# A two-layer hybrid block: transfers of the recurrence on the Sync queue, modulation weights loaded ahead, score matmuls over half the rows, another table of fillers

## The chip, the cores and the metric

The kernel runs on one core of one Trainium2 chip. The time is in device microseconds (us), smaller is better; each figure below says whether it is the median of the runs shown or one profiled execution. All data is float32 in HBM at the start, and the result is one tensor of 512x1024 float32.

## The reference, cut to what matters

Two layers, each over 256 context rows and 512 latent rows of width 1024. The second layer gives out only the latent rows.

```python
def trunk_layer(x, xc, c, c_ctx, last, ...):
    mod   = silu(c) @ w_mod + b_mod            # 6 vectors of 1024 (shift, scale, gate, twice)
    mod_c = silu(c_ctx) @ w_mod + b_mod        # the same for the context rows
    proj  = (x * (1 + sc1) + sh1) @ w_in       # parts: RWKV 1024, S5 256, q 512, k 128, v 128
    yr = rwkv_mixer(...)                       # 4 heads of 64; a state of 64x64, forward and reversed
    ys = s5_mixer(...)
    ya = attention_mixer(...)                  # 8 heads, 2 of keys; a band of 3 blocks of 128 and the context, with a sink
    mix = concatenate([yr, ys, ya]) @ w_out
    x = layer_norm(ALPHA * x + gt1 * mix, ln1_g, ln1_b)
    h = x * (1 + sc2) + sh2
    y = hier_moe(h, ...)                       # 4 groups of 8 experts, 2 experts a row, 3 matrices of 1024x512 each
    x = layer_norm(ALPHA * x + gt2 * y, ln2_g, ln2_b)
```

The recurrence of `rwkv_mixer` goes through all 768 rows, once in each direction: `s = s * w_t - (s kk_t) b_t + v_t k_t`, `y_t = s r_t`.

## The kernel before, in words

A layer has four stages, and the program records them one after the other.

1. `input_side` projects the rows with `w_in` (`proj`, matmul on line 243) and runs the S5 part; the RWKV part, the queries, the keys and the values go to HBM (`cvd`, `qd`, `kvd`, `yd`).
2. The mixing stage, where the change lies. `rwkv` works on 6 tiles of 128 rows. `front(i)` (line 366) makes the features of a tile and stores them in HBM records (`rec` line 461, `atd` line 462); `back(i)` (line 464) transposes them (tiles `ar`, `bz`), multiplies them into 64x64 score blocks (`sc`, matmul on line 503) and stores those too; `inverse(b)` inverts triangular blocks of 32 for three tiles and both directions at once, on VectorE and GpSimd; `solve(i, d)` reads its pieces back and stores the rest of the record (lines 571 to 610). Then `step(n, d)` (line 614) goes through 12 chunks of 64 rows for both directions: it loads a record of 512 KB (line 625) and does two small matmuls (lines 631 and 640) that depend on each other through the state; `output` (lines 672, 676) and `finish` make the rows from it. The transfers of these functions are issued in part by SyncE (SP), in part by ScalarE (ACT), whose sequencer then does no arithmetic until they are out.
3. The end of the mixing stage: `mixing` multiplies S5's and attention's part by `w_out` (`part`, line 1582, 12 matmuls of 512 columns a tile), later adds RWKV's part (`norm`, line 1635), does the first layer norm and the router (`choose`, whose counting matmul over `r_A` is on line 1458), and sorts the rows by expert (`finish`).
4. The experts: `Weights.fetch` (line 1824) loads three matrices of 2 MB for each of 32 experts on SP, `ffn_up` (line 1762) and `ffn_down` (line 1786) use them. The first six matrices lie in memory that the mixing stage has to give up first. `combine` and the second layer norm end the layer.

Between its pieces `rwkv` calls `fill(at)`, at the places 'front' (5 calls), 'back' (6), 'inverse' (1), 'step' (11) and 'end' (1). What a call records there is in the table `FILL`, for each layer three numbers a call: so many pieces of attention, so many units of modulation, so many pieces of `mixing`. A piece of attention is one pair of heads of a query tile: `scores` (matmul on line 877 of queries with keys), the softmax, and for the piece before it `turn` (transposes) and `values`. There are 24 pieces in layer 0 and 16 in layer 1. A unit of modulation (`mod_unit`) loads 512 KB of `w_mod` (tile `wmod`, line 118, two buffers), multiplies it (line 127) and reduces four partial sums (lines 135, 139); layer 0's mixing stage has 48 units (32 of layer 0, 16 of layer 1), layer 1's has 32. The keys lie in `kz` with 64 rows of zeros for each half of the heads, so that each score matmul goes over 128 rows; `bz` has zeros for the same reason.

The engines' orders inside the mixing stage come from a scheduler that the language runs over what was recorded: the places named here set what it may choose from.

```python
with tc.issue_after(k.load.ins):
    for _ in itertools.islice(att, n):
        pass
for q, c0 in itertools.islice(units, m):
    mod_unit(k, q, mp, c0, 128)
for _ in itertools.islice(mixes, x):
    pass
```

## Time and profile before

| what | us |
|---|---|
| median of 3 runs (2893.8 to 2897.02) | 2894.11 |
| the profiled execution's own time | 2882.98 |
| its span, first to last instruction | 2881.2 |

Busy time in the span: TensorE's matmuls 2219.2 us (77%), its weight loads 1487.5 us (52%, beside the matmuls), VectorE 1185.8 us (41%), GpSimd 823.0 us (29%), ScalarE 523.3 us (18%). 691.34 MB moved, 240 GB/s over the span. The shares are averages over stages that differ: from 273 to 930 us the core is in the mixing stage of layer 0, from 930 to 1485 in its experts, from 1823 to 2312 in the mixing stage of layer 1, from 2312 to 2835 in its experts. PE is TensorE's matmul, PEld its weight load, DVE VectorE, POOL GpSimd; a name with q (SPq, ACTq) is an engine's sequencer, which issues transfers.

### The profile page before, as it was taken

How to read it: one execution, taken by the hardware profiler on the slowest of the kernel's cores; microseconds unless marked ns; L12 is line 12 of the kernel's file. 1: busy time of each engine (PE TensorE's matmuls, PEld its weight loads, DVE VectorE, ACT ScalarE, POOL GpSimd, SP SyncE). 2: the span in 40 equal slices, each digit the busy share in tenths (PEclk: the TensorE clock that was granted, in tenths of full speed). 3: DMA queues.
4: the chain of work that ended last, by engine and by line, in shares of the span. 5: the costliest groups of instructions: out<-in, count | busy, mean ns of one | idle time of the engine just before them, and what ended most of it. 6: DMA issues, size and time to landing. Idle time of an engine off the chain costs nothing. (4 is left out here: it accounts for less than half of the span.)

```text
span 2881.2 us, 43454 instructions
## 1 busy us (share of the span) xinstructions
PE 2219.2 (77%) x16189; PEld 1487.5 (52%) x16189; DVE 1185.8 (41%) x2830; ACT 523.3 (18%) x1264; POOL 823.0 (29%) x1131
## 2 busy tenths in 40 slices
PE   5898677789874978989955787677898488788882
PEld 4786445567432544555525675455555254454441
DVE  7872554665556100000016873456645711111113
ACT  3222233223001100001015222233110100000001
POOL 2651322431544011101016652333324510111002
PEclk8999788789986999999987898579699699999996
DMA  8334466665627899989974324446784589998995
GB/s 241 93 94 116 141 179 185 175 189 163 220 93 265 351 418 371 391 329 379 388 279 121 83 56 142 117 128 161 212 244 140 230 355 418 416 379 331 384 419 201
DMA packets 404797, 691.34 MB, mean 240 GB/s; under 512 B 134755, under 2 KB 310627, under 8 KB 388097
## 3 DMA queue, kind: packets, MB, share of 16 engines
q1 hardware_dynamic: 311808, 600.10, 58.1%
q10 hardware_dynamic: 78880, 64.32, 7.5%
q0 software_dynamic: 13792, 22.61, 2.1%
q8 instruction: 211, 3.46, 0.5%
q14 instruction: 106, 0.86, 0.1%
HBM read 607.98 MB, written 95.44 MB: 244 GB/s over the span
## 5 line engine op out<-in xcount | busy, mean ns | idle before, releaser
L1762 PE MATMUL b_m<-w,xT 128*64 128x256 f32 x4928 | 593.7, 396 | 128.8 <-DMA w<-in_expert_w_gate_dram 80.2
L1762 PEld LDWEIGHTS b_m<-w,xT 128*64 128x64 f32 x4928 | 391.9, 142 | 333.3 <-issue 148.0
L243 PE MATMUL b_m<-xT,win 128*128 128x256 f32 (+1 forms) x1416 | 275.8, 355 | 7.0 <-POOL xT L167 3.5
L243 PEld LDWEIGHTS b_m<-xT,win 128*128 128x128 f32 x1416 | 232.8, 202 | 41.0 <-POOL xT L167 4.4
L1786 PE MATMUL b_m<-w,aT 128*64 128x512 f32 x1024 | 231.0, 592 | 1.1 <-issue 0.6
L1775 DVE COPY aT<-b_m 128x256 f32<-128x256 f32 x64 | 27.2, 425 | 474.4 <-PE b_m L59 474.4
L1792 POOL DMA_INDIRECT yb<-y,dx x64 | 63.9, 998 | 419.7 <-DVEq L1907 245.2
L1786 PEld LDWEIGHTS b_m<-w,aT 128*64 128x64 f32 x1024 | 76.2, 137 | 117.3 <-issue 108.3
L1764 ACT ACTIVATE act<-b_m 128x256 f32<-128x256 f32 x64 | 24.6, 384 | 566.8 <-PE b_m L1762 566.8
L1765 DVE TENSOR_TENSOR act<-act,b_m 128x256 f32<-128x256 f32 x64 | 27.0, 422 | 233.5 <-PE b_m L1762 233.5
L877 PE MATMUL b_a<-kz,qb 128*128 128x128 f32 (+2 forms) x416 | 111.9, 415 | 8.2 <-ACT pr L898 6.1
L1582 PE MATMUL b_a<-wo,yt 128*128 128x512 f32 x240 | 112.4, 618 | 0.0
L1792 POOL DMA_INDIRECT yb<-yo,dx x13 | 12.9, 994 | 291.7 <-ACTq L1907 166.2
L127 PE MATMUL b_a<-wmod,cc 128*32 128x128 f32 x1280 | 64.2, 315 | 40.0 <-DMA wmod<-in_w_mod_dram 28.0
L877 PEld LDWEIGHTS b_a<-kz,qb 128*128 128x128 f32 x416 | 78.2, 237 | 32.2 <-issue 13.0
L59 PE MATMUL b_a<-idf,pr 128*128 128x128 f32 x320 | 58.4, 304 | 34.3 <-DVE pt L921 11.5
L503 PE MATMUL b_g<-ar,bz 128*128 128x128 f32 (+1 forms) x384 | 66.2, 337 | 11.7 <-ACT bz L495 11.6
L1855 POOL DMA_INDIRECT xg<-hd,ix x32 | 33.0, 1031 | 146.8 <-PE b_m L59 105.2
L503 PEld LDWEIGHTS b_g<-ar,bz 128*128 128x128 f32 x384 | 61.8, 248 | 22.3 <-ACT bz L495 18.0
L1582 PEld LDWEIGHTS b_a<-wo,yt 128*128 128x128 f32 x240 | 45.2, 196 | 51.2 <-issue 50.3
L127 PEld LDWEIGHTS b_a<-wmod,cc 128*32 128x32 f32 x1280 | 37.7, 122 | 58.0 <-DMA wmod<-in_w_mod_dram 29.9
L551 POOL TENSOR_TENSOR tl<-Bm,Xh 112x4 f32<-112x4 f32 (+13 forms) x112 | 38.0, 339 | 95.0 <-DVE Xh L552 53.7
(539 smaller groups left out, 3979.9 us busy)
## 6 DMA issues: line engine op xcount, KB each, us to landing
w<-in_expert_w_gate_dram SPq DMA_DIRECT2D x64, 2048.0 KB
w<-in_expert_w_up_dram SPq DMA_DIRECT2D x64, 2048.0 KB
w<-in_expert_w_down_dram SPq DMA_DIRECT2D x64, 2048.0 KB
wmod<-in_w_mod_dram SPq DMA_DIRECT2D x80, 512.0 KB
rec<-rec SPq DMA_DIRECT2D x40, 512.0 KB
win<-in_w_in_dram SPq DMA_DIRECT2D x16, 1024.0 KB
wmod<-in_w_mod_dram SPq DMA_DIRECT2D x4, 2048.0 KB
sca<-sc SPq DMA_DIRECT2D x24, 256.0 KB
```

The source lines that it names most:

```text
L59: k.nc.tensor.transpose(out, x, k.idf[r:r + n, r:r + n])
L127: nc.tensor.matmul(p[32 * g:32 * g + 32, :], k.cc[:, kk, :], wt[:, kk, :], start=kk < 4, stop=kk >= 4, tile_position=(0, 32 * g))
L243: nc.tensor.matmul(p[:, :n], wt[u][:, kk, j * 128:j * 128 + 128], xT[v][:, kk, c0:c0 + n], start=kk == 0 and q == 0, stop=kk == 7 and q == 2)
L503: nc.tensor.matmul(pv[:, cp, q, 0:n, :], bk[:, hp, q, cp].rearrange("p s t -> p (s t)"), ar[:, 0:n, cp, q, :], start=True, stop=True)
L551: eng.tensor_tensor(t[:, 0:n, j:32], Bm[:, r0:r1, j:j + 1].to_broadcast([112, n, w]), x.to_broadcast([112, n, w]), op=ALU.mult)
L877: nc.tensor.matmul(dst, qb[:, 2 * v + e, :], kz[:, v, r, 128 * keys[c][0]:128 * keys[f - 1][0] + 128], start=c == 0 or (c == 4 and r == 0) ...
L1582: nc.tensor.matmul(ps[h], y[:, kt, :], wo[:, kt, 512 * h:512 * h + 512], start=kt == 0, stop=kt == 5)
L1762: mm = nc.tensor.matmul(p[64 * h:64 * h + 64, 0:256], xT[:, kk, :], w[:, kk, 256 * h:256 * h + 256], start=kk == 0, stop=kk == 7)
L1775: k.nc.vector.tensor_copy(aT, pa[:, 0:256].rearrange("p (j x) -> p j x", j=2))
L1786: nc.tensor.matmul(py[64 * s:64 * s + 64, :], aT[:, j, 64 * h:64 * h + 64], wd[:, q, 512 * s:512 * s + 512], start=q == 0, stop=q == 3)
L1792: sc = nc.gpsimd.indirect_dma_start(out=yb, out_offset=bass.IndirectOffsetOnAxis(ap=dst, axis=0), in_=y, in_offset=None, bounds_check=3071 ...
L1855: return nc.gpsimd.indirect_dma_start(out=out, out_offset=None, in_=hd, in_offset=bass.IndirectOffsetOnAxis(ap=idx, axis=0), bounds_check= ...
```

## The change: what it does

- Every transfer of `front`, `back`, `inverse` and `solve`, and the two small ones of `mod_unit`, that ACT issued is issued by SP. The store of `x1` in `norm` goes from SP to GpSimd.
- `mod_unit` is split: `mod_load` issues the load, and `fill` computes the units that the call before it loaded and then loads its own (at most 4), into four buffers of `wmod` in place of two. The loads are ordered behind the last transfer of RWKV, `k.latest`, that was recorded before. At 'end' what is left is loaded and computed at once.
- `kz` and `bz` lose their zeros: the two halves of the heads lie in rows 0 to 63 and 64 to 127, a score matmul goes over 64 rows, the two halves alternate and write to different PSUM banks.
- `FILL` is new. Pieces of attention in layer 0's front, back, inverse and step calls: 5, 6, 4 and 9 before, 5, 9, 3 and 7 after; units of modulation there: 12, 18, 6 and 12 before, 8, 12, 2 and 21 after, and 5 at 'end'. In layer 1 units: 0, 12, 9 and 11 before, 0, 12, 2 and 16 after, and 2 at 'end'; attention is unchanged there. Pieces of `mixing`: before, 2 in the sixth step call and 5 (layer 1: 3) in each from the eighth on; after, 1 in each from the fourth on and 2 in each of the last (three in layer 0). `mixing` does 4 (layer 1: 3) `w_out` parts before its router, 2 before.
- `pt`, the turned probabilities, has buffers by size.

```diff
-def mod_unit(k, l, mp, c0, n, bufs=2):
+def mod_load(k, l, mp, c0, n, bufs=2):
+    wt = mp.tile([128, 8, n], F32, name='wmod', bufs=bufs)
+    k.nc.sync.dma_start(wt, k.a['w_mod'][l].rearrange("(p k) n -> p k n", k=8)[:, :, c0:c0 + n])
+    return wt
+def mod_unit(k, l, mp, c0, n, wt):
...
-    bz = [Fp.tile([128, 2, 2, 2, 2, 64], F32, name='bz%d' % j) for j in range(2)]
+    bz = [Fp.tile([128, 2, 2, 2, 64], F32, name='bz%d' % j) for j in range(2)]
...
-            for src, r, c, q in ((kh[:, d], 0, 0, nc.scalar), (bt[:, d], 64, 0, nc.scalar), (VT[i], 0, 256, nc.sync)):
-                q.dma_start(rec[z, :, r:r + 64, c:c + 256], src)
-            nc.sync.dma_start(atd[z, :, 0], at[:, d, :])
+            for src, r, c in ((kh[:, d], 0, 0), (bt[:, d], 64, 0), (VT[i], 0, 256)):
+                nc.sync.dma_start(rec[z, :, r:r + 64, c:c + 256], src)
+            k.latest = nc.sync.dma_start(atd[z, :, 0], at[:, d, :])
...
-                for hp in range(2):
-                    r_ = slice(64 * hp, 64 * hp + 64)
-                    A.copy(bk[r_, hp, :, :, 1 - s, :], pv[r_])
+                A.copy(bk[:, :, :, 1 - s, :], p[:, 256 * s:256 * s + 256].rearrange("p (q c t) -> p q c t", q=2, c=2))
...
+            for q in range(2):
+                for cp in range(2):
+                    for hp in range(2):
+                        r_ = slice(64 * hp, 64 * hp + 64)
+                        nc.tensor.matmul(pvs[hp][:, cp, q, 0:n, :], bk[r_, q, cp].rearrange("p s t -> p (s t)"),
+                                         ar[r_, 0:n, cp, q, :], start=True, stop=True)
...
-        b = k.bank() if nk > 4 else None
+        b = [k.bank(), k.bank()] if nk > 4 else None
...
+        for c, f in runs:
+            for r in range(2):
+                q = slice(64 * r, 64 * r + 64)
+                dst = aa[r][:, 128 * c:128 * f] if c < 4 else b[r][:, 0:128]
+                nc.tensor.matmul(dst, qb[q, 2 * v + e, :], kz[q, v, 128 * keys[c][0]:128 * keys[f - 1][0] + 128],
+                                 start=c == 0 or c == 4, stop=True, skip_group_check=True)
...
-    for _ in range(2):
+    for _ in range(4 if l == 0 else 3):
         ready.append(parts.pop(0))
         part(ready[-1])
...
-            nc.sync.dma_start(x1[r], t)
+            G.dma_start(x1[r], t)
...
-                    for q, c0 in itertools.islice(units, m):
-                        mod_unit(k, q, mp, c0, 128)
-                    for _ in itertools.islice(mixes, x):
+                    for x in loaded:
+                        mod_unit(k, *x)
+                    loaded.clear()
+                    while True:
+                        with tc.issue_after(k.latest.ins):
+                            for q, c0 in itertools.islice(units, min(m, 4)):
+                                loaded.append((q, mp, c0, 128, mod_load(k, q, mp, c0, 128, 4)))
+                        if m < 9 or not loaded:
+                            break
+                        for x in loaded:
+                            mod_unit(k, *x)
+                        loaded.clear()
+                    for _ in itertools.islice(mixes, x_):
                         pass
```

What this does to the engines' orders is shown at three places. In these rows xN is a count of like instructions in a row, and a number behind a name tells buffers apart.

The first is ACT in layer 0's features, from the exponentials of one tile's features (L437 to L442, L440 to L445 in the change) to the next tile's sigmoids or scores. Before:

```order
L437 ACTIVATE e_3114<-e_3114 128x512
L438 ACTIVATE e_3115<-b_f 128x512
L442 ACTIVATE e_3119<-b_f 128x512
L474 DMA vz_2629<-rec 64x2x256
L129 COPY mres<-b_a 128x128
L461 DMA rec<-av 2x64x256
L461 DMA rec<-kd 2x64x256 x2
L461 DMA rec<-av 2x64x256
L894 ACTIVATE sm<-sm 128x2
```

The change:

```order
L440 ACTIVATE e_3053<-e_3053 128x512
L441 ACTIVATE e_3054<-b_f 128x512
L445 ACTIVATE e_3058<-b_f 128x512
L897 ACTIVATE sm<-sm 128x2
L901 ACTIVATE pr,s_3091<-b_a,sm 128x256 x2
L939 COPY ob<-b_a 128x256
```

Five transfers stood between the features and the softmax's first exponential (`sm`); none does now, and they stand in SP's order.

The second is PE at the end of layer 0's mixing stage, where the counting matmuls of the first `choose` (`r_A`, `tri`, `oneb`), `w_out` parts (`wo`, `yt`) and the last step's matmul of direction 0 (`b_f<-sb,rec` on L631, L632 in the change) follow each other. Before:

```order
L1462 MATMUL b_a<-r_A,oneb 128x32
L1582 MATMUL b_a<-wo_6766,yt 128x512 x36
L59 MATMUL b_f<-idf,y 128x128 x2
L713 MATMUL b_f<-g_2613,gl_4058 128x256
L672 MATMUL b_g<-sb_7471,rec_7521 64x128 x2
L1635 MATMUL b_a<-wo_7610,yo 128x512 x2
L59 MATMUL b_f<-idf,y 128x128 x2
L1635 MATMUL b_a<-wo_7610,yo 128x512 x2
L631 MATMUL b_f<-sb_7542,rec_7798 64x128 x2
```

The change:

```order
L632 MATMUL b_f<-sb_7407,rec_7651 64x128 x2
L1398 MATMUL b_a<-hT,wr 64x128 x4
L1585 MATMUL b_a<-wo_6251,yt 128x512 x2
L1398 MATMUL b_a<-hT,wr 64x128 x4
L1585 MATMUL b_a<-wo_6251,yt 128x512 x2
L1401 MATMUL b_a<-sel_108,r_lt 128x36
L1585 MATMUL b_a<-wo_6251,yt 128x512 x8
L1461 LDWEIGHTS tri
L1461 MATMUL b_a<-r_A,tri 128x32
```

The last step stands ahead of the first `choose` and of the two `w_out` parts that remain, one of which follows here; before, it stood behind `choose` and 36 matmuls of three parts.

The third is SP at the same end, up to the first expert's matrices. Before:

```order
L1576 DMA yt<-yd 128x768
L1578 DMA xq<-in_x_dram 128x1024
L1663 DMA x_0<-q 128x1024 x2
L1824 DMA w_7902<-in_expert_w_gate_dram 128x4096
L1824 DMA w_7904<-in_expert_w_up_dram 128x4096
```

The change:

```order
L1579 DMA yt<-yd 128x768
L1581 DMA xq<-in_x_dram 128x1024
L117 DMA wmod<-in_w_mod_dram 128x8x128 x4
L1652 DMA hd<-h 128x1024
L117 DMA wmod<-in_w_mod_dram 128x8x128
L1827 DMA w_7880<-in_expert_w_gate_dram 128x4096
L1827 DMA w_7882<-in_expert_w_up_dram 128x4096
```

Five loads of modulation and one store of `hd` now stand ahead of the first expert's matrices; the stores of `x1` are gone from there.

## Rows read from the trace of the kernel before

**Rows 1.** By stretch: us; PE, PEld, DVE, ACT, POOL busy; PE's clock; DMA share; GB/s.

```profile
273.00:561.00 288.00, 200.22 (x1658) 138.41 (x1659) 149.81 (x380) 89.52 (x273) 99.76 (x195) 0.78 0.59 164
561.00:771.00 210.00, 183.31 (x1804) 132.80 (x1802) 119.85 (x311) 50.52 (x169) 60.69 (x113) 0.89 0.68 198
...
843.00:930.00 87.00, 36.11 (x177) 22.17 (x176) 59.67 (x151) 9.57 (x19) 48.13 (x39) 0.65 0.59 211
930.00:1485.00 555.00, 488.72 (x3554) 285.05 (x3554) 49.04 (x107) 53.44 (x108) 61.69 (x61) 0.98 0.90 363
...
1823.00:2038.00 215.00, 166.58 (x1408) 124.94 (x1408) 127.33 (x317) 73.80 (x230) 74.42 (x164) 0.76 0.52 141
2038.00:2211.00 173.00, 149.22 (x1444) 95.38 (x1441) 90.77 (x211) 27.68 (x93) 60.00 (x85) 0.90 0.78 227
```

**Rows 2.** Instructions of ACT in time, 344 to 360 us: start, us, instruction, [idle before].

```profile
348.47 0.50 ACTq L461 DMA_DIRECT2D rec<-av  x1
...
353.91 4.59 ACTq L461 DMA_DIRECT2D rec<-av  x1
358.55 0.20 ACT L894 ACTIVATE sm<-sm 128x2 f32<-128x2 f32 x1 [10.12 <-DMA rec<-av]
```

**Rows 3.** Waits of ACT, 255 to 930 us: us in total, times, longest.

```profile
ACT mres L129 <- issue: 11.9, 2, 7.5
...
ACT mres L129 <- DMA rec<-av: 0.8, 1, 0.8
```

**Rows 4.** The same, 1810 to 2320 us.

```profile
ACT sm L894 <- DMA inv_t<-itm: 14.1, 1, 14.1
...
ACT xa L607 <- DMA xt<-inv_t: 1.3, 1, 1.3
```

**Rows 5.** Costliest groups of PE, whole span: busy us, mean ns, idle before and releasers.

```profile
L1786 PE MATMUL b_m<-w,aT 128*64 128x512 f32 x1024 | 231.0, 592 | 1.1 <-issue 0.6 <-DVE aT L1775 0.5
L1582 PE MATMUL b_a<-wo,yt 128*128 128x512 f32 x240 | 112.4, 618 | 0.0
L877 PE MATMUL b_a<-kz,qb 128*128 128x128 f32 (+2 forms) x416 | 111.9, 415 | 8.2 <-ACT pr L898 6.1 <-DVE qb L831 0.7 <-ACT pt L921 0.7
L503 PE MATMUL b_g<-ar,bz 128*128 128x128 f32 (+1 forms) x384 | 66.2, 337 | 11.7 <-ACT bz L495 11.6
L127 PE MATMUL b_a<-wmod,cc 128*32 128x128 f32 x1280 | 64.2, 315 | 40.0 <-DMA wmod<-in_w_mod_dram 28.0 <-ACT pr L898 10.7 <-DVE kd L431 0.6
```

**Rows 6.** Instructions of PE in time, 755 to 935 us.

```profile
802.32 0.21 PE L1458 MATMUL b_a<-r_A,tri 128*128 128x32 bf16 x1 [14.17 <-DVE r_A L1446]
...
802.47 33.34 PE L1582 MATMUL b_a<-wo,yt 128*128 128x512 f32 x72
...
840.83 0.32 PE L631 MATMUL b_f<-sb,rec 128*64 128x128 f32 x1
...
890.65 0.19 PE L1458 MATMUL b_a<-r_A,tri 128*128 128x32 bf16 x1 [7.77 <-DVE r_A L1446]
...
929.84 5.53 PE L1762 MATMUL b_m<-w,xT 128*64 128x256 f32 x34
```

**Rows 7.** The same, 2085 to 2330 us.

```profile
2093.66 0.64 PE L127 MATMUL b_a<-wmod,cc 128*32 128x128 f32 x16
2094.24 0.70 PE L877 MATMUL b_a<-kz,qb 128*128 128x256 f32 x2
...
2137.55 18.29 PE L1582 MATMUL b_a<-wo,yt 128*128 128x512 f32 x42
```

**Rows 8.** Issues of SP in time: around 340 us, and 860 to 935 us.

```profile
340.01 8.72 SPq L118 DMA_DIRECT2D wmod<-in_w_mod_dram  x2
349.19 0.81 SPq L462 DMA_DIRECT2D atd<-e  x2
...
871.70 0.33 SPq L1824 DMA_DIRECT2D w<-in_expert_w_gate_dram  x1
```

More of the change, by code (lines that the diff above doesn't have):

```diff
@@ L517, in back @@
             A.copy(r1, p[:, 0:256])
[L518 removed]
+            k.latest = nc.sync.dma_start(atd[z, :, 1], r1)
     def dblk(ap, s0, q):
@@ L919, in turn @@
                     tr(k, p[:, 256 * c + 128 * r:256 * c + 128 * r + 128], pr[:, r, 128 * (c0 + c):128 * (c0 + c) + 128])
-            t = P.tile([128, 512], F32, name='pt', bufs=6)
+            t = P.tile([128, 256 * n], F32, name='pt%d' % n, bufs=4 if n == 2 else 2)
             (A.copy if c0 % 4 else V.tensor_copy)(t[:, 0:256 * n], p[:, 0:256 * n])
```

84 lines of the change are left out of this document (36 added, 48 removed).

## The prediction, made before the changed kernel was run

> **What bounds the kernel now.** I read the busy times by stretch first, because the shares of the whole span mix stages that have nothing in common. In the experts' stretch the DMA share is 0.90 at 363 GB/s and PE is busy for 488.72 of 555 us [rows 1]: the matrices are the limit there, and the change touches nothing in it. Whatever moves must move in the two mixing stages, 273 to 930 us and 1823 to 2312 us. If such a stage ends earlier, the next one starts earlier, and the end of the kernel follows.
>
> Inside the mixing stage no single engine is the bound. In layer 0's features, 273 to 561 us, PE is busy for 200.2 of 288 us, DVE for 149.8, ACT for 89.5, and DMA has a share of 0.59 [rows 1]. That is a chain of waits through engines that each work in order. In the steps, 561 to 771 us, PE is busy for 183.3 of 210 us at a clock of 0.89 [rows 1]: there PE nearly is the bound, and what it does for others delays the recurrence. At the end, 843 to 930 us, it is busy for 36 of 87 us [rows 1]: norms, router and sorting, one after the other.
>
> Then I looked at what the queues do to these chains. ACT's time line shows it issuing stores of records: from 348.5 us on, four stores, and the softmax's small exponential behind them starts at 358.55, after 10.12 us without arithmetic [rows 2]. One store alone took 4.59 us to issue [rows 2], so the issue is held back. The table of ACT's waits shows how much there is of this in layer 0: 16 rows that name an issue or one of the transfers that the change moves, from 11.9 down to 0.8 us, add up to 88.5 us [rows 3] (I left out four whose transfer stays where it is). In layer 1 there are 13, from 14.1 to 1.3 us, in sum 84.4 us [rows 4]. The groups of instructions give what each matmul costs [rows 5], and PE's time line what stands in whose way [rows 6, 7].
>
> **The change part by part**, against the profiled execution, 2883.0 us; the median shown, 2894.1, is 11.1 us above it.
>
> *ACT issues no more transfers of RWKV.* Of the 88.5 us, 42.4 us are rows where the waiting instruction belongs to RWKV's own features or solves (the rest are attention's and modulation's); of the 84.4 us, 38.3 us. Together 80.7 us is the upper bound, nothing the lower. While one tile's chain stands still, another tile's matmuls and vector work go on, since two tiles are under way at a time; I take half: **-40**.
>
> *Modulation loaded one call ahead.* PE idled 28.0 us in front of L127 because `wmod` had not landed [rows 5]; in the features and the first steps the unit loads and multiplies in one call. With the load a call earlier and four buffers this can all go (-28), or nothing comes of it where the recurrence waits for something else (0). Half: **-14**. Nine more units in layer 0's steps cost PE 9 x 64.2/80 = 7 us, and three pieces of attention that leave the steps save 3 x 111.9/40 = 8 us in score matmuls alone. I set the two against each other.
>
> *Score matmuls over 64 rows.* L877 and L503 keep their count and columns. If the two halves run side by side, each pair takes the time of one. The trace has no pair of row halves of this size. The nearest rows are column halves: 512 columns cost 231.0/1024 = 0.226 us where halves alternate (L1786), and 112.4/240 = 0.468 us over the full array (L1582) [rows 5]. So the bounds are 0 and half of 111.9 + 66.2, 89 us. I take full overlap in busy time, and 40% of it on the path, since L877 lies partly in the steps (PE at 183.3/210 and 149.2/173) and partly, like all of L503, in features where PE has idle time (200.2/288, 166.6/215) [rows 1]: **-36**. A rule speaks against part of it. PE's order goes from modulation on 128*32 tiles straight into scores on 128*128: the first ends at 2094.30 and the second starts at 2094.24 [rows 7], with no idle time between the two. The Trainium skill, TensorEngine Tiling (Array Packing), Key Properties, says that a change of tiling mode drains the engine, and the change adds about 130 such passages, two for each of 40 pieces of attention and 24 tile-directions of `back`. By the row they cost nothing; by the rule, at an estimated 0.2 us each (about one matmul's own latency), the sum would be 26 us worse. The measurement shows no drain at such a passage, so I leave it at nothing.
>
> *`w_out` in steps.* Before, three parts (72 instructions, 33.34 us) run in one piece from 802.47 us on, after a wait of 14.17 us for the first `choose`, and the last step's matmul of direction 0 stands behind them at 840.83 us [rows 6]. In the new order that step stands ahead of `choose`, two of these parts have gone into earlier steps, and the last runs in a gap of the end. So 33.3 us leave the path behind `choose`, and two parts of 11.1 us come into steps in which PE is busy 87% of the time; I let 13 of those 22 us count: -20. In layer 1 a piece of 18.29 us between two steps [rows 7] is cut up the same way, and most of it only moves: -6. Sum **-26**; bounds 0 and -50.
>
> *Modulation left for the end.* Five units in layer 0 and two in layer 1 are loaded after the last step, ahead of the first expert's matrices on SP; the fifth needs a buffer that PE gives up behind the counting matmul of the second `choose`, 890.65 us, where the first matrix went out at 871.70 [rows 6, 8]. The cover is the time until the first expert's matmul at 929.84 [rows 6]: the six matrices that are fetched ahead, 12.6 MB at 363 GB/s [rows 1], take 35 us, and 890.65 + 35 = 926. If this cover goes, because the end gets shorter, each us is paid. I take 4 us in layer 0 and 2 in layer 1: **+6**; bounds 0 and 19 for the difference of the two issues, twice.
>
> *SP takes 232 transfers* (by the code: six for each of 24 tile-directions, 20 of `ar`, 12 of `vz`, 32 of modulation, 24 of `inverse`). At the 0.4 us or so of an issue that nothing holds back (two `atd` in 0.81 us [rows 8]), SP works 94 us more in the two stages. It does no arithmetic, but it works in order too: a store that waits for its producer holds up the next tile's loads. That was so before, where two loads of `wmod` held `atd` back from 340.0 to 349.2 us [rows 8]; those holds go with four buffers, and others come. No row shows SP with all of it. Bounds: 0, and the 80.7 us that ACT's chain now pays. I take somewhat over a third: **+30**.
>
> *Small ones.* 48 fewer copies into `bz` and half as many rotations of keys take work from ACT and DVE; the second score bank and a second reduction in 16 pieces add some. Net **-4**.
>
> Sum: -40 - 14 - 36 - 26 + 6 + 30 - 4 = -84. The profiled execution would take 2799, and the median, 11 us above it, **2810 us**.
>
> **The rivals.**
>
> *No overlap of the row halves.* Then the 36 us are missing: 2846. For it: the overlap is shown for column halves only. Against it: the weight loads and the banks differ for the two halves, as they do in L1786.
>
> *The clock.* The granted clock is 0.78 where PE is busy for 200.2 of 288 us, and 0.65 where it is for 36 of 87 [rows 1]: it lies between its two levels of 1.2 and 2.4 GHz, the lower the more often PE pauses. With 63 us less in the features PE pauses more. If the clock fell from 0.77 to 0.66 there, the remaining 304 us of PE work would take 51 us more, 40% of it on the path, 20 us: 2830. That goes with the Trainium skill, TensorE: Matmul & The Clock Gate, which says that the throttled state is the default and that activity releases it; by that rule I would give 2830, and the trace agrees as to direction.
>
> *The matrices wait for modulation.* If the end gets shorter by the 20 us of `w_out` while the last loads stay behind the second `choose`, the first expert waits for its matrices: up to 19 us in layer 0 and some 6 in layer 1, 2835.
>
> *SP becomes the bound, and the kernel slower.* A load of `wmod` is 512 KB, 3.2 us at 164 GB/s [rows 1], and now stands in the same queue as every record. If SP falls behind by a whole filler call, two such loads lie ahead of each store and read-back of a tile: two exposures of 6.4 us for each of six tiles, 77 us in layer 0, and about 50 in layer 1 with fewer loads. 2810 + 127 = 2937. It decides once the 94 us more of issues and the waits between them fill SP's idle time. [...] Against it: layer 0's features have 10 fewer units beside them (and inverse 4 fewer), 7 MB less.
>
> *Nothing comes out.* If the waits only change places, the time stays at 2890: the change does what it says, but chains go on through DVE and GpSimd, of which it takes little.
>
> **How the numbers follow.** The sum: 0.55. No overlap: 0.13. The clock: 0.08. Matrices wait: 0.10. SP the bound: 0.10. Nothing: 0.04. The prediction is that of the likeliest, 2810 us. Its own range is 2755 (ACT's whole 80.7 us, and half of what SP costs) to 2850 (no overlap). For 8 in 10 the upper end goes to 2885: it takes in the first three rivals and the larger price of SP, and leaves out the slower case and the one without effect, 14 in 100, and a little below. The lower end is 2745, 10 us below the likeliest's own, for `w_out`'s bound. A measurement of this kernel can tell about 0.2%, 6 us, from no change; so faster 0.86, the same 0.04, slower 0.10.
>
> **What would show it.** Right: ACT's waits on issues and on RWKV's transfers gone from its table (88.5 and 84.4 us to under 20); L877 and L503 at about half their busy time, 90 us in sum; PE's idle time for `wmod` under 8 us; no piece of `w_out` over 12 us ahead of a step; the first expert's matmul of layer 0 near 870 us instead of 929.84, and layer 1's mixing stage some 30 us shorter; the experts' stretches unchanged. Wrong: SP's own waits ahead of `cvt` or `rec` that grow by more than 50 us, PE waiting for `rec<-rec` in the steps, or the first expert waiting for `w` after its tokens have come.

## The result, and the profile after

The changed kernel takes 2976.69 us (median of 4 runs, 2973.61 to 2982.01), the kernel before 2893.95 on the same chip: a ratio of 1.029, 95% interval 1.0268 to 1.0311. It is 83 us slower; I had forecast 2810. The profiled spans are 2881.2 and 2976.6 us, 95.4 apart, since the profiled execution before was 11 us quicker than its median.

First by stretch, to be read against [rows 1]. The stretches of the kernel after are cut at the same events: first front to step 0's first matmul, steps of direction g, the last 87 us before the first expert, layer 0's experts, and the first two for layer 1. Columns as in [rows 1].

```profile
273.00:588.00 315.00, 195.04 (x1553) 131.41 (x1555) 165.62 (x405) 87.28 (x266) 100.25 (x204) 0.70 0.50 136
588.00:837.00 249.00, 198.58 (x1788) 134.23 (x1787) 109.77 (x281) 41.67 (x138) 52.51 (x97) 0.80 0.62 189
904.00:991.00 87.00, 41.73 (x242) 24.28 (x242) 47.62 (x138) 9.08 (x21) 39.43 (x35) 0.67 0.59 213
991.00:1546.00 555.00, 487.57 (x3552) 283.82 (x3554) 48.87 (x106) 53.21 (x107) 61.66 (x61) 0.98 0.90 363
1884.00:2115.00 231.00, 152.53 (x1376) 110.26 (x1378) 129.13 (x326) 69.10 (x219) 68.02 (x154) 0.73 0.51 142
2115.00:2314.00 199.00, 159.25 (x1442) 101.83 (x1442) 93.94 (x225) 24.36 (x80) 74.60 (x102) 0.79 0.65 194
```

The experts are unchanged (487.57 us of PE in 555). What was 288 us to the first step is now 315, with less PE work in it (195.04, was 200.22) at a lower clock (0.70, was 0.78); the steps, 210 us, now 249. These marks, read from PE's time line, tell where the 95 us arise:

| mark, us | before | after | more |
|---|---|---|---|
| layer 0: last store of the features | 507.3 | 507.4 | 0 |
| first matmul of step 0 | 561.8 | 587.7 | 26 |
| last step of direction g | 775.6 | 836.6 | 61 |
| first expert's matmul | 929.84 | 990.89 | 61 |
| layer 1: last matmul of the features | 1989.7 | 2036.0 | 46 |
| first matmul of step 0 | 2037.7 | 2114.9 | 77 |
| first expert's matmul | 2312.4 | 2405.0 | 93 |

The features themselves lose nothing, in layer 1 they gain 15 us (46 us late, after a start that is 61 us late). The loss lies between the features and the first step, 26 and 31 us, in layer 0's steps, 35, and in layer 1 from the first step to the first expert, 16.

PE's groups, as [rows 5], of the kernel after (line numbers there are 1 to 5 higher):

```profile
L880 PE MATMUL b_a<-kz,qb 64*128 64x128 f32 (+2 forms) x416 | 82.9, 447 | 57.1 <-DVE qb L832 55.1 <-DVE mrow L146 1.5 <-DMA qb<-qd 0.4
L59 PE MATMUL b_a<-idf,pr 128*128 128x128 f32 x320 | 68.8, 372 | 48.0 <-ACT pr L901 42.7 <-DVE pr L909 1.9 <-DVE mrow L146 1.6
L132 PE MATMUL b_a<-wmod,cc 128*32 128x128 f32 x1280 | 65.6, 310 | 20.1 <-DMA wmod<-in_w_mod_dram 11.0 <-ACT pr L901 3.2 <-DVE pt L924 2.9
...
L503 PE MATMUL b_g<-ar,bz 64*128 64x128 f32 (+1 forms) x384 | 37.8, 338 | 6.8 <-ACT bz L495 6.3 <-ACT ar L486 0.5
...
L516 PE MATMUL b_g<-vz,sc 128*64 128x64 f32 x384 | 27.8, 287 | 67.8 <-DVE sc L507 33.3 <-DMA vz<-rec 26.7 <-DVE Xh L553 4.4
```

and two groups of the kernel before that were not shown:

```profile
L59 PE MATMUL b_a<-idf,pr 128*128 128x128 f32 x320 | 58.4, 304 | 34.3 <-DVE pt L921 11.5 <-ACT pr L898 10.6 <-DVE pr L906 5.6
...
L515 PE MATMUL b_g<-vz,sc 128*64 128x64 f32 x384 | 25.6, 258 | 14.1 <-DVE sc L506 6.8 <-issue 5.1 <-DVE sm L904 1.8
```

Read the last column. PE now idles 57.1 us ahead of attention's scores, 55.1 of it for `qb`, whose sources SP loads (8.2 before, [rows 5]); 67.8 ahead of L516, 26.7 of it for `vz`, now an SP load (14.1 before); 48.0 ahead of the transposes of `pr` (34.3). Ahead of modulation it idles 20.1 (40.0 before). Together 96.4 us more idle time in four groups, while PE's busy time over the span fell from 2219.2 to 2210.7 us.

ACT's issue stalls did go, as forecast. Of the rows in [rows 3] that name an issue one is left in its table of waits, 255 to 1000 us (17.1 us, at L518). The longest wait for a transfer in layer 1, 1870 to 2410 us, is new:

```profile
ACT cvt L378 <- DMA cvt<-cvd: 31.9, 1, 31.9
```

It is not ACT's transfer but a load of `cvt` on SP that went out late. The waits moved to SP. Two rows of SP's table before, 255 to 930 us:

```profile
SPq L118 <- PE b_a L127: 71.8, 19, 21.9
...
SPq L610 <- DVE W L608: 15.1, 4, 4.4
```

and of its table after, 255 to 1000 us:

```profile
SPq L117 <- PE b_a L132: 94.3, 9, 30.7
SPq L610 <- ACT xa L608: 62.8, 9, 12.1
...
SPq L611 <- DVE W L609: 24.8, 4, 23.1
```

and its time line in two places, a burst of the features from 343 us on and the way to step 0 from 534 us on:

```profile
343.07 2.39 SPq L464 DMA_DIRECT2D rec<-av  x1
345.50 3.03 SPq L464 DMA_DIRECT2D rec<-vt  x1
348.58 2.60 SPq L465 DMA_DIRECT2D atd<-e  x1
351.23 3.00 SPq L117 DMA_DIRECT2D wmod<-in_w_mod_dram  x2
354.27 2.44 SPq L477 DMA_DIRECT2D vz<-rec  x1
356.82 0.54 SPq L488 DMA_DIRECT2D rec<-ar  x1
...
534.19 0.58 SPq L577 DMA_DIRECT2D x<-inv_out  x1
546.97 0.39 SPq L610 DMA_DIRECT2D rec<-xa  x1
547.45 0.60 SPq L611 DMA_DIRECT2D rec<-W  x1
548.11 0.60 SPq L577 DMA_DIRECT2D x<-inv_out  x1
548.76 0.60 SPq L579 DMA_DIRECT2D xt<-inv_t  x1
555.01 0.38 SPq L610 DMA_DIRECT2D rec<-xa  x1
...
562.20 0.37 SPq L610 DMA_DIRECT2D rec<-xa  x1
...
571.82 0.60 SPq L611 DMA_DIRECT2D rec<-W  x1
...
573.69 0.49 SPq L850 DMA_DIRECT2D qb<-qd  x1
574.23 1.82 SPq L856 DMA_DIRECT2D qr<-qd  x4
...
576.56 1.31 SPq L117 DMA_DIRECT2D wmod<-in_w_mod_dram  x2
577.91 1.47 SPq L626 DMA_DIRECT2D rec<-rec  x2
```

In the burst the rows follow each other and SP's table of waits is empty (339 to 358 us), and one issue still takes up to 3.03 us. The DMA share is 0.25 from 340 to 346 us and 0.17 from 346 to 352, so busy DMA engines don't explain it; what does isn't shown. In the second place SP stands for 12 us, from 534.8 to 546.97, in front of a store whose producer, ACT's copy into `xa`, isn't done; loads of the next solves (`x`, `xt`) stand behind that store, and so on for four solves. The first load of a record goes out at 577.91, behind the outputs of four solves, the second inverse's loads, a query's loads and two `wmod`. Before it went out at 544.51. And the query's loads at 573.69 are what PE waits for: its scores at 584.74 have 13.74 us of idle time for `qb` ahead of them, and step 0's matmul stands behind them in PE's order.

### The profile page after: what moved, and what is told of

It is laid out like the page before. It is cut to its first block, busy times and chain, and to the rows that moved or that the text cites. A ratio compares the mean times of both kernels' runs of the same rounds, so it can differ in the third digit from the quotient of the medians.

```text
span 2976.6 us, 43375 instructions
## 1 busy us (share of the span) xinstructions
PE 2210.7 (74%) x16189; PEld 1466.1 (49%) x16189; DVE 1192.4 (40%) x2828; ACT 509.4 (17%) x1216; POOL 822.9 (28%) x1131
## 5 line engine op out<-in xcount | busy, mean ns | idle before, releaser
L880 PE MATMUL b_a<-kz,qb 64*128 64x128 f32 (+2 forms) x416 | 82.9, 447 | 57.1 <-DVE qb L832 55.1
L59 PE MATMUL b_a<-idf,pr 128*128 128x128 f32 x320 | 68.8, 372 | 48.0 <-ACT pr L901 42.7
L880 PEld LDWEIGHTS b_a<-kz,qb 64*128 64x128 f32 x416 | 50.0, 243 | 76.9 <-DVE qb L832 56.1
L59 PEld LDWEIGHTS b_a<-idf,pr 128*128 128x128 f32 x320 | 52.3, 193 | 57.6 <-ACT pr L901 46.3
L132 PE MATMUL b_a<-wmod,cc 128*32 128x128 f32 x1280 | 65.6, 310 | 20.1 <-DMA wmod<-in_w_mod_dram 11.0
L657 POOL TENSOR_TENSOR sn<-st,gc 128x128 f32<-128x128 f32 x44 | 25.2, 576 | 197.5 <-DVE st L648 186.8
L516 PE MATMUL b_g<-vz,sc 128*64 128x64 f32 x384 | 27.8, 287 | 67.8 <-DVE sc L507 33.3
L937 PE MATMUL b_a<-pt,vta 128*64 128x256 f32 x320 | 61.1, 483 | 5.3 <-DVE pt L924 4.6
```

Of the source, the lines that this page charges most:

```text
L59: k.nc.tensor.transpose(out, x, k.idf[r:r + n, r:r + n])
L132: nc.tensor.matmul(p[32 * g:32 * g + 32, :], k.cc[:, kk, :], wt[:, kk, :], start=kk < 4, stop=kk >= 4, tile_position=(0, 32 * g))
L516: nc.tensor.matmul(p[64 * cp:64 * cp + 64, 64 * h:64 * h + 64], sc[:, 0, cp, hp, q, :], vv[:, cp, 64 * h:64 * h + 64], start=True, stop=True)
L880: nc.tensor.matmul(dst, qb[q, 2 * v + e, :], kz[q, v, 128 * keys[c][0]:128 * keys[f - 1][0] + 128], start=c == 0 or c == 4, stop=True, ski ...
L937: nc.tensor.matmul(o[64 * v:64 * v + 64, 0:256], vt[:, keys[c][0], 64 * v:64 * v + 64], PT[v, c // 2][:, 256 * (c % 2):256 * (c % 2) + 256 ...
```

## The experiments

Each ratio is to runs of the kernel before on the same chip. Of the 232 transfers moved, 104 are the features' (`front`, `back`), 96 those of the inverses and solves, 32 modulation's. (Two expectations miscount: that of the first run says 232 where it puts back RWKV's 200, that of the run with one store says 84 for the 96.)

**Undo one part of the change.** The queue put back (such a line for each of RWKV's transfers that the change moved):

```diff
-        nc.sync.dma_start(rec[z, :, :, 512:640].rearrange("c p x -> p c x"), xa)
+        nc.scalar.dma_start(rec[z, :, :, 512:640].rearrange("c p x -> p c x"), xa)
```

> The changed kernel with RWKV's 232 transfers back on ACT's queue where they were (the two transfers of modulation stay on Sync). Theory 1, Sync's one queue: stores that wait for their producers hold up the next tile's loads and the first record's load; then layer 0's first step starts 25 us earlier (587.7 back to about 562), layer 1's 30 us earlier after the same shift, direction g's chain of steps takes 214 us instead of 249, and the time falls by 60 to 90 us, to 2887 to 2917. Rival, the filler table: the time falls by less than 20 us, 2957 or more, since the same fillers still stand ahead of the steps. Rival, a trade: ACT's stalls on issues come back (17 to 88 us in its table of waits) and eat up the gain, within 10 us of 2977.

Measured 0.9997 (0.997 to 1.0024): 85 us of 2895 come back with RWKV's 200 transfers alone, all of the loss; modulation's 32 stay on SP. Layer 0's step 0 starts at 543.3 us, 18 earlier than before the change.

Only the table's third column put back:

```diff
-    for _ in range(4 if l == 0 else 3):
+    for _ in range(2):
```

> The changed kernel with only the table's third column, the pieces of w_out and norm, as before (two, none, then five pieces per step, and two tiles ahead instead of four or three). Theory 2, the pieces of the end go out too slowly: the stretch from the last step of direction f to the first expert's matmul in layer 0 goes from 129 back to about 90 us, and the time falls by 30 to 45 us, to 2932 to 2947. Rival, Sync's queue alone: the last tiles of attention and of the recurrence arrive late for other reasons, and the time stays within 10 us of 2977.

Measured 1.0273 (1.0239 to 1.0307): no difference. Theory 2 falls. The whole table put back (`FILL` as before, and the loop of `fill` to serve it):

```diff
-                        if m < 9 or not loaded:
+                        m -= 4
+                        if m <= 0 or not loaded:
```

> The changed kernel with the whole table of fillers as before (attention, modulation and end), loads still one call ahead where a call has at most four units (a call of more loads four at a time, the last four ahead). If attention beside the features is what delays the fronts and the first step (PE waits for the softmax there, 48 us ahead of b_a<-pr where it was 34), the time falls by 60 to 95 us, to 2882 to 2917, more than with the end's column alone. If Sync's queue is what delays them, it falls only by what the end's column gives, 0 to 45 us, and layer 0's first step stays at 580 us or later.

Measured 1.0359 (1.0322 to 1.0397), slower still, which neither branch had; step 0 starts at 620.3 us. Attention beside the features, as the new table has it, isn't what delays the fronts.

**One part of the change alone**, on the kernel before. Its queue edit for RWKV's 200 transfers only:

> The kernel before with RWKV's transfers on Sync as the only edit (modulation's loads still two buffers deep, unit by unit, in the same queue). If one in-order queue is the cause by itself, as in the run that put them back (74 us), this costs 50 to 100 us: 2945 to 2995. If it only hurts together with the new order of fillers and loads, it costs under 25 us, and if my prediction's sum was right without them it gains 10 us: 2884 to 2919.

Measured 1.0318 (1.0293 to 1.0344), 92 us slower. The queue alone does it, with the old table, buffers, keys and modulation. The keys and the block tile without zeros only:

```diff
-    kz = P.tile([128, 2, 2, T], F32, name='kz')
+    kz = P.tile([128, 2, T], F32, name='kz')
...
-                nc.tensor.matmul(dst, qb[:, 2 * v + e, :], kz[:, v, r, 128 * keys[c][0]:128 * keys[f - 1][0] + 128],
+                nc.tensor.matmul(dst, qb[q, 2 * v + e, :], kz[q, v, 128 * keys[c][0]:128 * keys[f - 1][0] + 128],
```

> The kernel before with only the keys and the block tile without zeros (score matmuls over 64 rows, two banks for the fifth key tile). By the prediction's term for the score matmuls, with the small ones: 2854 (minus 40), and L877's group of matmuls at about half its 111.9 us of busy time. If the halves don't overlap: 2890 to 2894. If each change of tiling mode costs a drain (130 passages at an estimated 0.2 us): 2880 or up to 2920.

Measured 1.0046 (1.0025 to 1.0067): 13 us slower instead of 40 faster. With the loads one call ahead in four buffers as well (and `pt` by size):

> The kernel before with the keys without zeros (whose room the four buffers need) and modulation loaded one filler call ahead in four buffers, with before's table and RWKV's transfers on ACT; to be compared with the keys alone, 2912. My term for the loads ahead was 14 us with bounds 0 and 28: 2884 to 2912, PE's 30.5 us idle for wmod under 10. Rival: before's table asks for more than four units in some calls, the load stands behind the step's record load by the new edge, and nothing comes of it: 2905 to 2920.

Measured 1.0067 (1.0044 to 1.009), no gain. PE still idles 25.1 us for `wmod`.

**Which transfers.** From the changed kernel, parts of the queue edit undone, by lines as in the first diff. The 96 of the second half (`itm`, `inv_out<-itm`, two of `inv_t`, `atl`, `xt`, `rec<-xa`):

> The changed kernel with only the solves' and inverses' transfers of the second half back on ACT (block loads, inverse stores, the solve's two loads, its first output); the features' transfers stay on Sync. With all of RWKV's transfers back the time fell by 74 us. If the hold is between the solves' outputs and the records' loads, this gives most of it: layer 0's first step at about 565 us instead of 588, steps some 30 us shorter, 2915 to 2935. If it is in the features, where a tile's stores stand in front of the next tile's loads, 2960 to 2980.

The 104 of the features (`rec<-kd`, `rec<-av`, `vz`, `rec<-ar`, `atd<-r`):

> The counterpart: the changed kernel with only front's and back's transfers back on ACT, the solves' and inverses' on Sync. If the hold is in the features, layer 0's features end some 12 us earlier than at 507 us and PE no longer waits for the read-back of v (15.5 us in one piece); 2915 to 2935. If it is between the solves' outputs and the records' loads, 2950 to 2970. If both parts count about alike, this and the run before each give 30 to 45 us, 2932 to 2947.

Measured 1.0054 (1.0028 to 1.0079) and 1.0202 (1.017 to 1.0235), 2915.56 and 2952.48 us: 68 and 25 us of the 85, as the second half's theory had it. In the first, the record load goes out at 549.1 us and step 0 starts at 559.0. So the second half carries most. Then one waiting store alone, the line of the first diff and nothing else:

> The changed kernel with one store alone, each solve's first output (rec from xa, 24 of the 232 transfers), back on ACT. If the 62 us that putting back the second half's 84 transfers gave come from this one store, which waits 62.8 and 54.8 us at the head of Sync's queue for ACT's copies while the next solve's loads and the records' loads stand behind it, the time falls by 40 to 62 us: 2915 to 2937. If they come from the solve's loads standing behind other stores, or from the number of transfers, it falls by less than 20 us: 2957 or more.

Measured 1.0272 (1.0247 to 1.0296), 5 us, within the intervals. My theory of the one store fell, and SP's table of waits of this kernel, 255 to 1000 us, shows what took its place:

```profile
SPq L611 <- DVE W L609: 69.0, 10, 17.6
```

The store beside it, which waited 24.8 us, now waits 69.0 in the same place. Both outputs off SP:

```diff
+        nc.scalar.dma_start(rec[z, :, :, 512:640].rearrange("c p x -> p c x"), xa)
+        nc.scalar.dma_start(rec[z, :, 64:128, 256:512].rearrange("c t x -> t c x"), W[64:128])
```

> The changed kernel with both outputs of each solve (rec from xa and from W, 48 transfers) on ACT; the solves' loads and the records' loads stay on Sync, with the features' stores. If loads that stand behind stores that wait for their producers are the cause, this gives most of the 62 us of the second half: 2915 to 2935, and layer 0's first record load goes out near 550 us instead of 577.9. If the length of the order of loads on Sync is the cause, or its place in the program's order, less than 20 us: 2957 or more.

The solves' loads off, the outputs left:

```diff
+        nc.scalar.dma_start(at, atd[z])
+        nc.scalar.dma_start(t[u:u + 32], inv_t[s0:s0 + 8].rearrange("h i t -> i h t"))
```

> The changed kernel with each solve's two loads (inverse, second half, and at with its product, 48 transfers) back on ACT, the outputs on Sync. If loads behind waiting stores are the cause, this gives part of the 62 us, since the records' loads still stand behind the outputs: 20 to 45 us, 2932 to 2957. If it is the number of issues of Sync, 48 of 232 give a fifth of 74 us, 15 us: 2962.

Measured 1.0211 (1.0178 to 1.0244), 23 us, 2953.67, between the two ranges that I had given, and 1.0281 (1.0253 to 1.031), nothing, above both of its. 48 issues fewer gave 23 us in one and nothing in the other, so the number of issues alone isn't the cause. Step 0 starts at 579.3 and 594.0. In both the record's load still stands behind the second inverse's and the query's loads. So I left everything on SP and wrote the records' loads earlier:

```diff
     solves(0, 0)
+    load(0)
+    load(1)
     solves(0, 1)
...
         steps((n,))
+        if n < 11 and n != 5:
+            load(n + 1)
```

> The changed kernel, every transfer on Sync as changed, with the records' loads written earlier in the program: those of steps 0 and 1 right behind the first solves, the others one step ahead, before the fillers' loads. If the place in Sync's order is the cause, the first record load goes out near 552 us instead of 577.9, layer 0's first step starts 15 to 25 us earlier, layer 1's too, and the time falls by 30 to 60 us: 2917 to 2947. If the steps are late because the solves themselves are late (their own loads and stores wait in turn), the loads go out early but PE waits for rec, and the time falls by less than 15 us: 2962 or more.

Measured 1.0266 (1.0241 to 1.0291). It did what was meant. SP's time line of this kernel (L624 is the record's load):

```profile
558.80 0.40 SPq L624 DMA_DIRECT2D rec<-rec  x1
...
579.64 0.57 SPq L863 DMA_DIRECT2D qb<-qd  x1
580.25 1.81 SPq L869 DMA_DIRECT2D qr<-qd  x4
```

and PE's (L649 is step 0's matmul, L893 attention's scores):

```profile
565.59 0.46 PE L649 MATMUL b_f<-rec 128*64 128x64 f32 x8 [0.34 <-DVE W L609]
...
571.61 0.63 PE L586 MATMUL b_g<-xt,ab 32*32 32x32 f32 x8 [4.10 <-DMA xt<-inv_t]
...
590.74 2.51 PE L893 MATMUL b_a<-kz,qb 64*128 64x256 f32 x16 [13.15 <-DVE qb L845]
```

The record load goes out 19 us earlier and step 0 starts 22 us earlier, at 565.59. But the query's loads now go out at 579.64 where it was 573.69, PE waits 13.15 us for them again, and behind them wait the next solves. Layer 0's last steps come earlier as well, direction g's by 19 us and f's by 25. But the first `choose` comes at 881.13 us where it was 880.35, and the first expert only 5 us earlier: the end of the stage didn't follow the steps, and what holds it wasn't tried. In layer 1 step 0 comes 23 us earlier and the first expert 8 later. So the time is as in my second case, though step 0 doesn't wait for `rec`. Neither this order nor any of the partial ones on one queue gave the time back.

**The rest of the change, without the queue edit.** RWKV's transfers on ACT; layer 1's row of the table and layer 0's third column as before (`range(2)`):

> The changed kernel with RWKV's transfers on ACT, layer 1's row of the table as before, and the end's pieces of layer 0 as before; keys without zeros, loads one call ahead and layer 0's attention and modulation as changed. If the 33 us that layer 1's mixing stage lost in the run with the queue put back come from the table, layer 1 returns to about 542 us of mixing and the time to 2860 to 2875, faster than before. If they come from the keys (the granted clock), it stays at 570 us and 2895 to 2905.

and with layer 1's row alone as before:

```diff
-        {'front': ((1, 0, 0),), 'back': ((0, 2, 0), (1, 2, 0)), 'inverse': ((1, 2, 0),),
...
+        {'front': ((1, 0, 0), (1, 0, 0)), 'back': ((0, 0, 0), (1, 4, 0), (1, 2, 0), (1, 2, 0)), 'inverse': ((1, 9, 0),),
...
-    for _ in range(4 if l == 0 else 3):
+    for _ in range(4 if l == 0 else 2):
```

> The changed kernel with RWKV's transfers on ACT and only layer 1's row of the table as before; layer 0 keeps the changed table, the end's pieces too. If the stages add up, layer 0 takes the 637 us of mixing of the run with the queue put back and layer 1 the 542 us of the mixed run: 2902 minus 33, 2869, the fastest so far. If layer 0's pieces only move the wait (its tail was 131.8 us after the last step where it was 86.8), 2885 to 2895.

Measured 0.9977 (0.9959 to 0.9994) and 0.9919 (0.99 to 0.9937). The second, 2872.73 us, is the fastest version and beats both kernels. Layer 1's mixing stage, first front to first expert, takes 541.7 and 541.4 us in the two, as expected, and 574.6 with the changed row (which of the row's columns costs it wasn't tried). The first version missed its 2860 to 2875 by layer 0, where the old third column takes 657 us of mixing and the new one 639.

With two modulation buffers and two loads ahead in place of four, and then with the zeros of the keys on top:

```diff
-                                loaded.append((q, mp, c0, 128, mod_load(k, q, mp, c0, 128, 4)))
-                        m -= 4
+                                loaded.append((q, mp, c0, 128, mod_load(k, q, mp, c0, 128, 2)))
+                        m -= 2
```

> The fastest version (RWKV's transfers on ACT, layer 1's row as before, keys without zeros) with modulation in two buffers, two loads ahead, as in the run with zeros (2920). If the zeros cost that run its 47 us, this stays near 2873, within 10 us. If the two buffers cost them, this is at 2905 to 2925 and the zeros cost nothing. PE's idle time for wmod tells how much of it the buffers are: 18.1 us in the fastest version, 28.3 in the run with zeros.

> The fastest version so far (2873: RWKV's transfers on ACT, layer 1's row as before) with the keys' zeros as before, so attention's score matmuls over 128 rows again; for the room, modulation in two buffers, two loads ahead. If the 64-row matmuls cost by the clock that PE is granted, as the keys alone did (13 to 17 us), this is faster: 2855 to 2865, with PE's clock in layer 0's features back from 0.74 to about 0.79. If they gain once PE is the bound of the steps, as my sum had it, this is 20 us slower: 2885 to 2900.

Measured 1.0041 (1.0025 to 1.0058) and 1.0089 (1.0055 to 1.0123). So in this setting four buffers are worth 35 us (PE idles 44.6 us ahead of modulation with two, 29.7 with four) and the keys without zeros 14, though the two intervals touch. My expectation of the run with zeros missed with both branches (2920.14 us), since I had put the two buffers at nothing; that of the two buffers came out, but for the zeros costing nothing.

All six parts of `w_out` in layer 0's steps, from the third filler call on:

```diff
-    for _ in range(4 if l == 0 else 2):
+    for _ in range(6 if l == 0 else 2):
```

> The same fastest version (keys without zeros, four buffers) with layer 0's six parts of w_out all in steps 2 to 7, so that none stands between the last step and the router. The tail after the last step of direction f is 133.6 us there and was 86.8 before; two parts of about 10 us each stand in it between two chooses that are 41 us apart. If those parts are the wait, the tail shrinks by 25 to 40 us, the steps grow by 10 to 20: 2850 to 2865. If DVE's and ACT's norms set the 41 us, the steps grow and the tail stays: 2880 to 2890.

Measured 0.9945 (0.9924 to 0.9966), no better than without. PE's time line of the fastest version, the three `choose` and the first expert:

```profile
810.01 0.21 PE L1461 MATMUL b_a<-r_A,tri 128*128 128x32 bf16 x1 [11.04 <-DVE r_A L1449]
...
852.58 0.18 PE L1461 MATMUL b_a<-r_A,tri 128*128 128x32 bf16 x1
...
894.08 0.21 PE L1461 MATMUL b_a<-r_A,tri 128*128 128x32 bf16 x1 [4.65 <-DVE r_A L1449]
...
917.22 8.02 PE L1765 MATMUL b_m<-w,xT 128*64 128x256 f32 x64
```

and of the version with six parts:

```profile
831.82 0.19 PE L1461 MATMUL b_a<-r_A,tri 128*128 128x32 bf16 x1 [5.01 <-DVE r_A L1449]
...
874.89 0.19 PE L1461 MATMUL b_a<-r_A,tri 128*128 128x32 bf16 x1 [13.23 <-DVE r_A L1449]
...
896.29 0.21 PE L1461 MATMUL b_a<-r_A,tri 128*128 128x32 bf16 x1 [4.65 <-DVE r_A L1449]
...
917.92 7.38 PE L1765 MATMUL b_m<-w,xT 128*64 128x256 f32 x60
```

The tail after the last step shrank from 133.6 to 98.5 us, but the steps grew by 35, and the first expert starts at the same time. In both it comes 22 to 23 us behind the third `choose`, right behind the copy into its tokens' tile `xT`, so it doesn't wait for its matrices. What sets the time of the third `choose` stays open.

Last, the price of score work by itself: every 64-row score matmul twice, on the kernel with the keys alone (and in `back` the loop over `q` as `(0, 1, 0, 1)`).

```diff
-        for c, f in runs:
+        for c, f in runs + runs:
```

> The keys-alone kernel with every score matmul over 64 rows issued twice (the second run overwrites the first's result), for PE's busy time of before without its waits. If the keys alone lost their gain to the granted clock (0.75 in the steps where it was 0.89, 0.69 in the features where it was 0.79) because PE has less to do, the clock here goes back above 0.85 in the steps and the time does not rise: 2895 to 2912. If the clock is low because matmuls over half the rows count for less, it stays near 0.75 and the time goes up by the added work on the path, 15 to 45 us: 2927 to 2957.

Measured 1.02 (1.0171 to 1.0229), 45 us slower than with the keys alone. A stretch of layer 0's steps that begins 10 us ahead of step 0, columns as in [rows 1], of the keys alone:

```profile
548.00:776.00 228.00, 195.34 (x1775) 137.47 (x1775) 110.77 (x307) 50.54 (x169) 57.13 (x112) 0.75 0.61 177
```

and of the doubled one:

```profile
561.00:800.00 239.00, 209.92 (x2036) 154.99 (x2036) 127.12 (x349) 56.77 (x188) 67.48 (x132) 0.81 0.63 187
```

Doubling adds 83 us of busy time (93.8 + 41.4 to 140.8 + 77.0), so 1 us of score work costs half a us on the path, near the 40% that I had taken. The granted clock was 0.89 before [rows 1], 0.75 with less score work, and 0.81 with more than before, where PE is busy for 209.92 of 239 us, as large a share as before: it came back half way. The time rose as the second theory had it, the clock did not do what either had, so neither is shown. What lowers it isn't settled, nor how much of the time it costs.

## Why the prediction was wrong

The steps of my sum, put beside a path from before to after in which each kernel adds one part:

| kernel | ratio | this part, us | predicted |
|---|---|---|---|
| keys and blocks without zeros | 1.0046 | +13 | -40 (scores, small ones) |
| and loads ahead, four buffers | 1.0067 | +6 | -14 |
| and layer 0's attention and modulation, `x1` on GpSimd | 0.9977 | -26 | 0 |
| and layer 0's `w_out` in steps | 0.9919 | -17 | -20 |
| and layer 1's row | 0.9997 | +23 | -6 |
| and the queue | 1.029 | +85 | -10 |

(The us are the difference of two ratios times 2895, uncertain by 6 to 10 us each. My +6 for modulation left for the end belongs to the rows of the table.)

*The queue: the step that failed.* I had set -40 for ACT against +30 for SP. Two things were wrong. First, "at the 0.4 us or so of an issue that nothing holds back": I took the quickest issues. Summed over the issues in the two mixing stages (255 to 930 and 1765 to 2312 us before, 255 to 991 and 1826 to 2405 after), SP spent 298 us before and 511 after, 213 more and not 94: 151 for the transfers that had been ACT's, 0.65 us each, and 62 more for those that were SP's already. ACT had spent 154 us on the same transfers, so the trace before had their price; its 4.59 us for one store [rows 2] I had charged to ACT alone. Second, the price of the waits: I bounded SP's loss by what ACT's chain pays, "0, and the 80.7 us", and took a third. A wait at the head of SP's queue holds loads of other chains (queries, records, `cvt`), which had stood on SP behind fewer such stores, so that upper bound wasn't one. How the 85 us divide between the longer issues and these holds isn't shown. The -40 was real in the table of waits and worth nothing in time: with the queue on ACT (0.9997) ACT's waits on issues and on these transfers are back, 52.2 us in 12 rows of its table in layer 0, and the kernel is 85 us faster. I had also read too much into that table: 16.4 of the 80.7 us are waits for transfers that SP issued before too (`rec<-vt`, `x<-inv_out`, `wmod`, `inv_out<-Xh`). The Trainium skill says in DMA: Bandwidth & Descriptors, Issuing engines are not separate DMA queues, that issuing on several engines saves only the sequencer's time to initiate, usually small. The runs differ from that: the same transfers on two engines are worth 85 to 92 us. In the trace an issue that waits holds back all that stands behind it on its engine, 12 us at 534.8; that such holds are all of the difference isn't shown.

*SP becomes the bound* was the rival with the right sign, at 0.10. Its mechanism was half right. On the way to step 0 no load of `wmod` waits; SP waits for ACT's `xa`, 26.8 us in layer 0 (507 to 588 us) and 28.1 in layer 1, and query loads stand ahead of the records. In layer 0's steps SP does wait 53.7 us in front of `wmod`, but that was 61.5 before; what is new there is 36.0 us for `xa`, and 24.3 for `W` where it was 15.1. Its 127 us, on top of 2810, were less than the 167 us by which the forecast failed, since the other gains failed too.

*Score matmuls.* The halves run side by side, as I had assumed, so *no overlap* falls: in 331 of the 400 pairs the second half starts within 12 ns of the first. At a granted clock of 1.0 (2.4 GHz) the next pair over 128 columns follows after 105 ns, where a full-row score matmul followed after 112; at 0.5 (1.2 GHz) the two are 207 and 213. Yet busy time fell only from 111.9 to 82.9 us (L880) and from 66.2 to 37.8 (L503), 57 us and not 89. Counted from start to start the two groups took 139.4 us before and 78.4 after; the rest, the last matmul of each run of them up to its end as the profile models it, stayed (39.0 and 42.8). So the term was too large in busy time because that last matmul doesn't halve, and little of it was gained on the path: nothing is seen on the kernel before (+13), and 14 us in the fastest version with two buffers. Of the rivals, the clock fell as it said: with the keys alone from 0.79 to 0.69 in the features (255 to 561 us; I had written 0.77 to 0.66) and from 0.89 to 0.75 in the steps. Of the steps from one of attention's 128-column score matmuls, or pairs, to the next 73 of 182 were slow ones (213 ns) before, 74 of 131 with the keys alone. Whether that is what cost the gain isn't shown.

The drain: I read "no idle time between" two modes as no cost. That was the wrong comparison. Over successive matmuls that overlap in the two mixing stages before, at a granted clock of 1.0, a full-array matmul over 128 columns is followed after 111 ns (median) if the next has the same tile size and after 203 if it has another; over 512 columns, after 429 and 522. At 0.5 it is 213 and 351, 854 and 991. So a change costs about 0.09 us, at the lower clock 0.14. The Trainium skill says in TensorEngine Tiling (Array Packing), Key Properties, that a change of tiling mode drains the engine; the trace agrees, with those 0.09 and 0.14 us. The price here is small: from one matmul to the next the size changes 587 times in the two stages before and 679 times with the keys alone, 92 times 0.09 to 0.14, 8 to 13 us, not 26.

*Modulation ahead.* Alone nothing, as its lower bound had it; together with the new row of layer 0, 35 us. (Of the 8 us that I had set against the nine more units, a third wasn't there: two pieces of attention leave the steps, not three.) *`w_out` in steps* was right for layer 0 (-17, forecast -20) and not for layer 1, whose row as a whole costs 23 us; PE's time line there still has pieces of 13.02 and 9.71 us ahead of steps. With the queue on SP the column is worth nothing (1.0273 without it). *The matrices wait for modulation* falls, and no run shows the +6: in the changed kernel the first expert's matmul at 990.89 us starts right behind DVE's copy into `xT`, and its six matrices had been issued from 929.9 to 960.6.

Of the signs that I named, two came out: ACT's issue stalls nearly gone, the experts unchanged. `w_out` was cut up but for one piece of 13.02 us. Missed were `wmod` at 11.0 us where I wanted under 8, the score groups at 120.7 us in sum where I wanted 90, and both signs of an earlier end (the first expert near 870 us, layer 1's mixing stage 30 us shorter). Two of "wrong" came out: PE waits for `rec` in the steps (15.3 us, was 3.0), and SP's waits in front of stores into `rec` grew by more than 50 us (62.8 for `xa` in layer 0 and 54.8 in layer 1).

## What to carry to other kernels

A queue works in order, so moving an issue off a busy engine moves its wait to whatever is next on the other queue; before moving, list for the target what would stand behind each store that waits for a producer, and price issues by their mean in bursts, not by the quickest. With all on one queue, neither taking out its longest wait nor writing one load earlier gave the time back here (5 and 7 us of 85); only moving whole chains to the second queue did (68 us for the solves'). And the worth of a part depends on what else waits: four buffers gave nothing on one version and 35 us on another.

## What the runs showed of the hardware

Row halves of 64x128 tiles in two banks run side by side: the second starts within 12 ns of the first, and the next pair over 128 columns follows after 105 ns at a granted clock of 1.0 (207 at 0.5), where a full-row one is followed after 112 (213). Busy time fell less, from 111.9 to 82.9 us for 416 matmuls, as the last matmul of a run keeps its length. A change of tile size between full-array matmuls and others costs 0.09 us at a granted clock of 1.0 and 0.14 at 0.5. An issue on SP in a burst without waits takes from 0.41 to 3.03 us, the longest of them at a DMA share of 0.25 and 0.17 (340 to 352 us). The granted clock fell by 0.14 in a stretch (0.89 to 0.75) in a kernel with less work for PE; how much time that cost isn't shown.
